# A forgetting attention that leaves its softmax undivided: the division moved to the outputs, the queries negated, the tiles moved

## The chip, the cores and the metric

The kernel is one program on one core of a Trainium2 chip. The metric is the device time of one execution in microseconds (us). A core has TensorE (PE in the profile, with PEld for its weight loads), VectorE (DVE), ScalarE (ACT), GpSimd (POOL) and SyncE (SP), which issues all of this kernel's DMAs from one in-order queue. Data lives in on-chip SBUF (128 partitions), matrix products land in PSUM (8 banks of 512 float32 in each partition), and everything else is in DRAM.

## The reference

The reference is a decoder trunk of two layers over 1024 tokens of 1024 features: convolution layer, cross-attention into 256 memory tokens, MLP; then forgetting attention, cross-attention, MLP; then a final norm. The change lies in the forgetting attention. With 16 heads of 64 features, queries `q`, keys `k`, values `v` and `c`, the cumulative sum of the log forget gates:

```python
s = jnp.einsum("bqhd,bkhd->bhqk", qi, k).astype(jnp.float32) * scale
s = s + (ci[..., :, None] - c_bhs[:, :, None, :])
s = jnp.where(mask[None, None], s, -jnp.inf)      # causal
p = jax.nn.softmax(s, axis=-1)
return jnp.einsum("bhqk,bkhd->bqhd", p.astype(v.dtype), v)
```

The result, over all heads, is multiplied by `w_o` and added to the stream. The term with `ci` is the same for a whole row and drops out of the softmax.

## The kernel before

**Number format.** Each float32 operand of a matrix product is split into a high part (ACT copies it, rounded to fp32r) and a low part (DVE subtracts: line 153, in `low`, called by `split`), and three products are summed (line 268, or 1246 in the attention's projections).

**Attention (`attend`).** The loop runs over 16 heads and, in each, over 8 blocks of 128 queries. `attention_scores` makes the scores of one block, 512 keys at a time, on PE (lines 1296 and 1297, and 1299 for the causal mask, which is added as a product with the identity). One custom DVE operation (line 1301) subtracts `cj`, the heads' gate sums broadcast over the partitions, and keeps the running row maximum `mx`. DVE negates it (`nb`, line 1304). ACT takes the exponential with that bias and sums the row into `rs` (line 1306). DVE inverts the sum (1307) and multiplies the whole row by it (1312); in odd blocks of the last two heads ACT does that (1310). `attention_transposes`, three blocks later, turns the probabilities on PE (1332) and splits them (`pth` by ACT at 156, `ptl` by DVE at 153). `attention_output`, one step after that and once for two blocks, multiplies by the values (1344, 1345), adds the two halves of the PSUM tile (1347 on ACT, 1348 on DVE) and stores `ol` to `od` in DRAM (1350). Between the blocks the loop takes three steps of `projections`, the keys, queries and values of later heads (L1246), which read the normalized stream from eight large tiles `op`.

**After it (`fox_layer`).** The eight `op` tiles are taken again for the attention's output: for each chunk `m` of 128 features (heads 2m and 2m+1) and each half of the tokens, a tile `o` is loaded from `od` (1138) and split into `op`. Then the stream is loaded again (`load_x`, line 138, from `xd`), into the place where the attention's own tiles were, and `linear_by_halves` multiplies by `w_o`: first half of the tokens for all eight output chunks, then the second half. One output chunk and half is 24 products, over eight `op` tiles in turn; its weights are two tiles `wh` and `wl`, two buffers each, and the sums go through six PSUM banks.

**What sets the order.** A planner in the compiler takes the program as traced, and issues on each engine the earliest instruction in the program that is ready by its own estimates; the order is then fixed. The MLPs are an exception: their order is written out by hand. Tiles of one tag share its buffers. The tag `t` of the pool `nrm` has four buffers of 128x512, used all over the kernel; in the attention only by `mask`, and after it by `o`. In this program each tag `t` tile is first written in the order in which the program asks for it.

**Places in SBUF.** The planner stacks the tiles of a pool in steps of 32 bytes. An unused tile `shift` of 64 bytes, set to zero at the start, stands first in the pool `nrm`. With it the tiles of `nrm`, the `op` tiles and the tiles of the MLPs begin at multiples of 128 bytes in each partition; the tiles of the attention (pool `fa`), behind the 4 bytes of `fb`, begin 32 or 96 bytes past such a multiple; the stream's tiles `x` begin 224 bytes past a multiple of 256, and the weight tiles `raw`, `wh`, `wl` 192 bytes past one.

Of the kernel before, what the change touches and what calls it, by code (L numbers as in the profile page):

```python
# [12 lines left out]
F32 = mybir.dt.float32  # L13
F32R = mybir.dt.float32r
AF = mybir.ActivationFunctionType
ALU = mybir.AluOpType
# [3 lines left out]
P = 128  # L20
D = 1024
S = 1024
NCH = D // P
HALF = 512
# [4 lines left out]
HEADS = 16  # L29
HD = 64  # L30
# [6 lines left out]
HALVES = (slice(0, HALF), slice(HALF, S))  # L37
# [49 lines left out]
def trunk(ctx, tc, a, out):  # L87
    nc = tc.nc
    act, dve, pool, pe = nc.scalar, nc.vector, nc.gpsimd, nc.tensor
# [14 lines left out]
    def col(name, i):  # L104
        return par[:, COLS[name] + i : COLS[name] + i + 1]

    def shift(p):

        dve.memset(p.tile([P, 16], F32, name="shift", bufs=1), 0.0)

    @contextmanager
    def in_order(engines=None):

# [25 lines left out]

    X = open_x()  # L140
    nrm = ctx.enter_context(tc.tile_pool(name="nrm", bufs=2))
    shift(nrm)
    opool = ctx.enter_context(tc.tile_pool(name="ops", bufs=8))
    ps = ctx.enter_context(tc.tile_pool(name="ps", bufs=2, space=PSUM))

    def bank(p):
        return p.tile([P, HALF], F32, name="mm", tag="mm")
# [7 lines left out]
    def split(hi, lo, src):  # L155
        act.copy(hi, src)  # L156
        low(lo, src, hi)
# [944 lines left out]
    def fox_layer(xd, hs, ws, seconds):  # L1102
        nonlocal X, xpool
        cd = dram.tile([HEADS, S], F32, name="cd")
        od = dram.tile([NCH, P, S], F32, name="od")

        early = {}
        with (
            tc.tile_pool(name="fs", bufs=2, space=PSUM, reuse_waits="tile") as p2,
            banks(4) as pm,  # L1110
        ):

            with in_order({mybir.EngineType.PE, mybir.EngineType.DVE, mybir.EngineType.Activation}):
# [12 lines left out]
                early["gate"] = bank(pm)[:HEADS, :]  # L1126
                product(early["gate"], by_weights(wf, hs, HALVES[0]))
                normalize(hs, None, HALVES[1], rb)
                ws.append(weights(a["wv"][0], gain="kv"))
            xpool.close()  # L1130
            xpool = ExitStack()
            with tc.tile_pool(name="fa", bufs=2) as bp:
                attend(bp, p2, pm, ws, wf, hs, early, cd, od)
        hs = operands()
        for m in range(NCH):
            for sl in HALVES:
                o = nrm.tile([P, HALF], F32, name="o", tag="t", bufs=4)
                nc.sync.dma_start(o, od[m, :, sl])
                split(*(x[:, sl] for x in hs[m]), o)
        X = open_x()  # L1140
        for sl in HALVES:
            load_x(X, xd, sl)
        with banks(6) as pm:
            linear_by_halves(pm, lambda m: weights(a["fox_wo"][m]), NCH, hs, add_to_x)

    def attend(bp, p2, pm, ws, wf, hs, early, cd, od):
        mask = nrm.tile([P, P], F32, name="mask", tag="t", bufs=4)
        make_causal_mask(nc, mask, mask_val=-1e30)
        maskr, identr = (bp.tile([P, P], F32R, name=n, bufs=1) for n in ("maskr", "identr"))
        dve.tensor_copy(maskr, mask)  # L1150
        dve.tensor_copy(identr, ident)
        tiles = {}
        project = projections(bp, ws, hs, tiles, early)
        gates = forget_gates(bp, wf, hs, cd, early)
        next(gates)
        while len(tiles) < 2:
            next(project)
            next(gates, None)
        late = []

        def run(late):
            later = []
            for n, f in late:
                if n == 0:
                    f = f()
                    if f:
                        later.append((DELAYS[1], f))
                else:
                    later.append((n - 1, f))
            return later  # L1170

        for head in range(HEADS):
            cj = bp.tile([P, S], F32, name="cj")
            nc.sync.dma_start(cj, cd[head : head + 1, :].to_broadcast([P, S]))
            for b in range(8):
                while head not in tiles:
                    next(project)
                x = attention_scores(bp, p2, tiles[head], head, b, cj, identr, maskr)
                late.append((DELAYS[0], partial(attention_transposes, bp, pm, tiles[head], head, b, x, od)))
                late = run(late)  # L1180
                for _ in range(3):
                    next(project, None)
        while late:
            late = run(late)

    def forget_gates(bp, wf, hs, cd, early):

        fb = bp.tile([HEADS, 1], F32, name="fb", bufs=1)
        nc.sync.dma_start(fb, a["fb"])
        z, e, w = (bp.tile([P, S], F32, name="x", bufs=DELAYS[0] + 1)[:HEADS, :] for _ in range(3))  # L1190
        cn = bp.tile([P, S], F32, name="cj")[:HEADS, :]
        for sl in HALVES:
            if sl.start == 0:
                t = early["gate"]
            else:
                t = bank(ps)[:HEADS, :]
                product(t, by_weights(wf, hs, sl))
            dve.tensor_scalar(z[:, sl], t, fb[:, 0:1], None, op0=ALU.add)
        yield
        act.activation(e, z, AF.Abs)  # L1200
        yield
        act.activation(e, e, AF.Exp, scale=-1.0)
# [12 lines left out]
        yield  # L1215
        dve.scalar_tensor_tensor(z, z, 0.0, cn, op0=ALU.min, op1=ALU.subtract)
        yield
        dve.tensor_tensor_scan(cn, z, z, 0.0, op0=ALU.add, op1=ALU.bypass)
        nc.sync.dma_start(cd, cn)
# [43 lines left out]

    def put_queries(bp, sl, t, qs):
        q = bp.tile([P, HALF], F32, name="q", tag="qv")
        act.activation(q, t, AF.Copy, scale=1.0 / math.sqrt(HD))  # L1266
        for i, (mine, other) in enumerate(ROWS):
            split(qs[i][mine, sl], qs[i][other, sl], q[mine, :])

# [12 lines left out]

        return transposed

    def attention_scores(bp, p2, tiles, head, b, cj, identr, maskr):

        kh, kl, qs, _, _ = tiles
        n = (b + 1) * P
        x = bp.tile([P, S], F32, name="x", bufs=DELAYS[0] + 1)
        qb = qs[:, b * P : (b + 1) * P]  # L1290
        mx = -3e38
        for j in range(0, n, HALF):
            sl = slice(j, min(j + HALF, n))
            last = sl.stop == n
            s = bank(p2)[:, : sl.stop - j]
            pe.matmul(s, qb, kl[:, sl], start=True, stop=False)  # L1296
            pe.matmul(s, qb, kh[:, sl], start=False, stop=not last)
            if last:
                pe.matmul(s[:, b * P - j :], identr, maskr, start=False, stop=True)
            m = bp.tile([P, 1], F32, name=f"mx{j}")  # L1300
            dve.tensor_tensor_reduce(x[:, sl], s, cj[:, sl], 1.0, mx, ALU.subtract, ALU.max, m)  # L1301
            mx = m
        nb = bp.tile([P, 1], F32, name="nb")
        dve.tensor_scalar(nb, mx, -1.0, None, op0=ALU.mult)  # L1304
        rs = bp.tile([P, 1], F32, name="rs")
        act.activation(x[:, :n], x[:, :n], AF.Exp, bias=nb, accum_out=rs)  # L1306
        dve.reciprocal(rs, rs)
        if head >= HEADS - 2 and b % 2:

            act.activation(x[:, :n], x[:, :n], AF.Copy, scale=rs)  # L1310
        else:
            dve.tensor_scalar(x[:, :n], x[:, :n], rs, None, op0=ALU.mult)
        return x

    def attention_transposes(bp, pm, tiles, head, b, x, od):
# [121 lines left out]
```

## Time and profile before

| what | value |
|---|---|
| median of three runs | 2830.04 us (2828.89 to 2830.18) |
| profiled execution: its own time | 2829.92 us |
| profiled execution: span in the trace | 2827.8 us |
| PE busy | 2749.2 us (97%) |
| DVE busy | 2024.9 us (72%) |
| ACT busy | 1275.5 us (45%) |
| granted TensorE clock, mean | 0.994 |

All times in the trace count from the start of its span; the run's own time is 2.1 us longer than the span. The attention runs from about 1388 us to 1893 us. The trace shows a product's duration with its latency: products of 512 columns last 393 ns, though one follows the other in less, so a busy PE can still have room. A row of the grouped view reads: line, engine, operation, output<-inputs, shape, count, then busy time and mean duration, then the engine's idle time just before, and what ended it.

### The profile page before, as it was taken

The numbers are of one execution on the slowest core, as the hardware profiler recorded it, in microseconds if no ns is written. First come the engines' busy times: TensorE is split into PE (matmuls) and PEld (weight loads), VectorE is DVE, ScalarE is ACT, GpSimd is POOL, SyncE is SP. The second block draws the span as 40 slices with busy tenths as digits, with TensorE's granted clock in tenths as the row PEclk, the third lists the DMA queues.
The fourth block names the chain that finished last, engine by engine and source line by source line (L and its number), as shares of the span: only waits on it lengthen the run. The fifth ranks groups of instructions, "written<-read, shape, count | busy, mean of one in ns | idle before, by whom it ended". The sixth has DMA issues, their size and how long they took to land.

```text
span 2827.8 us, 36219 instructions
## 1 busy us (share of the span) xinstructions
PE 2749.2 (97%) x12968; PEld 2256.6 (80%) x12968; DVE 2024.9 (72%) x3359; ACT 1275.5 (45%) x2293; POOL 705.3 (25%) x473
## 2 busy tenths in 40 slices
PE   8999999999999999999899999989999999999998
PEld 6777777888788877878588888878888888878886
DVE  5999983555766576777788888884545855577776
ACT  5112143433465553334466666673423655543332
POOL 0000000000065625774000000000000365625763
PEclk9999999999999999999999999999999999999999
DMA  6334463322164585652222222133322355565651
GB/s 219 119 119 134 124 204 119 97 90 82 53 224 177 184 303 192 215 196 88 68 73 72 65 60 59 61 120 114 97 67 102 140 187 190 196 231 195 227 201 60
DMA packets 165428, 390.68 MB, mean 138 GB/s; under 512 B 17264, under 2 KB 46192, under 8 KB 164992
## 3 DMA queue, kind: packets, MB, share of 16 engines
q1 hardware_dynamic: 165248, 388.37, 40.5%
q8 instruction: 102, 1.67, 0.2%
q14 instruction: 78, 0.64, 0.1%
HBM read 270.79 MB, written 113.31 MB: 136 GB/s over the span
## 4 chain that ended last, share of the span: by engine, by line
PE 73%; DVE 14%; ACT 5%; DMA 4%; issue 3%; SPq 0%; POOL 0%; DVEq 0%; POOLq 0%; ACTq 0%
PE mm L1066 35%; PE mm L268 27%; PE mm L1246 5%; DVE x L407 2%; DVE op L153 2%; DVE w L153 2%; PE mm L1332 1%; DVE x L1301 1%; PE mm L1344 1%; PE mm L1345 1%; DVE both L399 1%; ACT x L1306 1%; DVE wl L153 1%; DMA ua<-x 1%; PE mm L1296 1%
## 5 line engine op out<-in xcount | busy, mean ns | idle before, releaser
L1066 PE MATMUL mm<-op,w 128*128 128x512 f32 x5424 | 1253.0, 393 | 19.1 <-DVE w L153 5.7
L1066 PEld LDWEIGHTS mm<-op,w 128*128 128x128 f32 x5424 | 1019.9, 188 | 248.7 <-DVE w L153 6.5
L268 PE MATMUL mm<-op,wh 128*128 128x512 f32 x1056 | 332.4, 396 | 2.5 <-DVE op L153 2.5
L153 DVE TENSOR_TENSOR w<-r,w 128x512 fp32r<-128x512 f32 x264 | 260.9, 992 | 32.8 <-ACT w L651 32.8
L651 ACT CAST w<-r 128x512 fp32r<-128x512 f32 x264 | 162.4, 620 | 262.7 <-PE mm L1066 229.0
L268 PEld LDWEIGHTS mm<-op,wh 128*128 128x128 f32 x1056 | 200.2, 190 | 47.7 <-DVE op L153 3.8
L1246 PE MATMUL mm<-op,wh 128*128 128x512 f32 x736 | 229.5, 393 | 0.0
L153 DVE TENSOR_TENSOR w<-t,w 128x512 fp32r<-128x512 f32 x180 | 177.2, 997 | 64.7 <-ACT w L651 64.5
L268 PE MATMUL mm<-op,wl 128*128 128x512 f32 x528 | 210.5, 400 | 9.7 <-DVE x L965 8.9
L212 POOL TENSOR_TENSOR r<-v,mhalf 128x4 f32<-128x4 f32 (+1 forms) x15 | 16.8, 1117 | 749.6 <-DVE v L210 749.6
L645 POOL TENSOR_TENSOR t<-r,t 128x512 f32<-128x512 f32 x104 | 171.5, 1649 | 92.3 <-DVE w L153 65.6
L156 ACT CAST wh<-raw 128x1024 fp32r<-128x1024 f32 x96 | 100.6, 1049 | 197.6 <-PE mm L268 100.6
L863 POOL TENSOR_TENSOR x<-x,x 128x512 f32<-128x512 f32 x112 | 161.2, 1464 | 113.1 <-ACT x L876 102.3
L651 ACT CAST w<-t 128x512 fp32r<-128x512 f32 x180 | 111.7, 620 | 163.8 <-PE mm L1066 140.3
L965 DVE TENSOR_TENSOR x<-mm,x 128x512 f32<-128x512 f32 x160 | 109.4, 684 | 94.2 <-PE mm L1066 77.0
L1246 PEld LDWEIGHTS mm<-op,wh 128*128 128x128 f32 x736 | 138.7, 188 | 26.4
L268 PE MATMUL mm<-op,xsh 128*128 128x512 f32 x512 | 157.7, 392 | 0.0
L1246 PE MATMUL mm<-op,wl 128*128 128x512 f32 x368 | 154.9, 421 | 1.8 <-ACT q L1266 1.8
L156 ACT CAST pth<-mm 128x512 fp32r<-128x512 f32 (+1 forms) x224 | 105.8, 495 | 108.8 <-PE mm L555 79.7
L645 POOL TENSOR_TENSOR t<-r,r 128x512 f32<-128x512 f32 x52 | 81.7, 1571 | 292.9 <-DMA r<-in_ff_w 253.9
L407 DVE SCALAR_TENSOR_TENSOR x<-d,par,x 128x512 f32<-128x512 f32 x232 | 154.5, 745 | 0.0
L1306 ACT ACTIVATE x<-x,nb 128x128 f32<-128x128 f32 (+7 forms) x128 | 99.5, 778 | 107.7 <-DVE nb L1304 100.7
(189 smaller groups left out, 4681.8 us busy)
## 6 DMA issues: line engine op xcount, KB each, us to landing
r<-in_ff_w SPq DMA_DIRECT2D x128, 512.0 KB, 4.0
op<-ua SPq DMA_DIRECT2D x80, 512.0 KB, 6.7
us<-x SPq DMA_DIRECT2D x128, 256.0 KB, 2.9
op<-us SPq DMA_DIRECT2D x64, 512.0 KB, 5.4
raw<-mvo SPq DMA_DIRECT2D x32, 512.0 KB, 3.3
ua<-ul SPq DMA_DIRECT2D x64, 256.0 KB, 2.1
ua<-uh SPq DMA_DIRECT2D x60, 256.0 KB, 2.2
raw<-in_pw SPq DMA_DIRECT2D x24, 512.0 KB, 4.7
```

The source lines that it names most:

```text
L153: dve.tensor_tensor(lo, src, hi.bitcast(F32), op=ALU.subtract)
L156: act.copy(hi, src)
L268: pe.matmul(out_ps, x, y, start=i == 0, stop=i == len(terms) - 1)
L399: dve.scalar_tensor_tensor(both, odd[:, j : j + n], sums[:, j : j + 1], both, op0=ALU.mult, op1=ALU.add)
L407: dve.scalar_tensor_tensor(out[s], d[:, j : j + n], w, y, op0=ALU.mult, op1=ALU.add)
L645: (dve if g in (2, 3, UP, UP + 1) else pool).tensor_tensor(t, raws[g, x], raws[g, y], op=ALU.subtract)
L651: act.copy(highs[n][0], raws[steps[n][:2]])
L863: eng.tensor_tensor(u[g, x], y1, y2, op=op_)
L965: dve.tensor_tensor(v, sums[key], v, op=ALU.add)
L1066: pe.matmul(sums[key], y, z, start=first and i == 0, stop=n == last_of[key] and i == len(terms) - 1, skip_group_check=True,)
L1246: pe.matmul(t, x, y, start=n == 0, stop=n == len(terms) - 1)
L1306: act.activation(x[:, :n], x[:, :n], AF.Exp, bias=nb, accum_out=rs)
```

## The change

The scores are computed negated: `put_queries` scales by -1/8, the mask is +1e30, the DVE operation adds `cj` and keeps the row minimum, and ACT takes the exponential with scale -1 and that minimum as its bias. So the negation of the maximum falls away. The row sums go into a column of one tile `rs` of 128x16 for two heads, and neither the inversion nor the division of the rows is done there. Instead `inverse_sums`, once for two heads, inverts the 128x16 sums on DVE, transposes them on PE, copies them on ACT to a tile `ro` (of the tag `t`) and stores them to `rd` in DRAM. After the attention each tile `o` is multiplied by a tile `rs` (also of the tag `t`), which two DMAs fill, one for each head, broadcast over 64 partitions. That loop now runs over the halves outside and the chunks inside. The 64 bytes of `shift` are gone, so that `nrm`, the `op` tiles and the MLPs' tiles begin 64 bytes lower; `fb` takes 128 bytes a partition and the row minima have four buffers, so that all large tiles of the attention begin 64 bytes past a multiple of 128.

```diff
-    def shift(p):
-        dve.memset(p.tile([P, 16], F32, name="shift", bufs=1), 0.0)
...
-    shift(nrm)
...
+        rd = dram.tile([HEADS, 8, P], F32, name="rd")
...
-        for m in range(NCH):
-            for sl in HALVES:
+        for sl in HALVES:
+            for m in range(NCH):
                 o = nrm.tile([P, HALF], F32, name="o", tag="t", bufs=4)
                 nc.sync.dma_start(o, od[m, :, sl])
+                r = nrm.tile([P, HALF], F32, name="rs", tag="t", bufs=4)
+                for i in range(2):
+                    blocks = rd[2 * m + i : 2 * m + i + 1, sl.start // P : sl.stop // P, :]
+                    nc.sync.dma_start(
+                        r[i * HD : (i + 1) * HD, :], blocks.rearrange("h b q -> h (b q)").to_broadcast([HD, HALF])
+                    )
+                dve.tensor_tensor(o, o, r, op=ALU.mult)
                 split(*(x[:, sl] for x in hs[m]), o)
...
-        make_causal_mask(nc, mask, mask_val=-1e30)
+        make_causal_mask(nc, mask, mask_val=1e30)
...
+        def inverse_sums(pair, rs):
+            dve.reciprocal(rs, rs)
+            t = bank(pm)[:16, :P]
+            pe.transpose(t, rs, ident)
+            o = nrm.tile([P, HALF], F32, name="ro", tag="t", bufs=4)[:16, :P]
+            act.copy(o, t)
+            nc.sync.dma_start(rd[2 * pair : 2 * pair + 2, :, :].rearrange("h b q -> (h b) q"), o)
...
+            if head % 2 == 0:
+                rs = bp.tile([P, 16], F32, name="rs")
...
+                k = head % 2 * 8 + b
+                x = attention_scores(bp, p2, tiles[head], b, cj, identr, maskr, rs[:, k : k + 1])
...
+            if head % 2:
+                inverse_sums(head // 2, rs)
         while late:
             late = run(late)
...
-        fb = bp.tile([HEADS, 1], F32, name="fb", bufs=1)
+        fb = bp.tile([HEADS, 32], F32, name="fb", bufs=1)[:, :1]
...
-        act.activation(q, t, AF.Copy, scale=1.0 / math.sqrt(HD))
+        act.activation(q, t, AF.Copy, scale=-1.0 / math.sqrt(HD))
...
-            m = bp.tile([P, 1], F32, name=f"mx{j}")
-            dve.tensor_tensor_reduce(x[:, sl], s, cj[:, sl], 1.0, mx, ALU.subtract, ALU.max, m)
-            mx = m
-        nb = bp.tile([P, 1], F32, name="nb")
-        dve.tensor_scalar(nb, mx, -1.0, None, op0=ALU.mult)
-        rs = bp.tile([P, 1], F32, name="rs")
-        act.activation(x[:, :n], x[:, :n], AF.Exp, bias=nb, accum_out=rs)
-        dve.reciprocal(rs, rs)
-        if head >= HEADS - 2 and b % 2:
-            act.activation(x[:, :n], x[:, :n], AF.Copy, scale=rs)
-        else:
-            dve.tensor_scalar(x[:, :n], x[:, :n], rs, None, op0=ALU.mult)
+            m = bp.tile([P, 1], F32, name=f"mn{j}", bufs=4)
+            dve.tensor_tensor_reduce(x[:, sl], s, cj[:, sl], 1.0, mn, ALU.add, ALU.min, m)
+            mn = m
+        act.activation(x[:, :n], x[:, :n], AF.Exp, bias=mn, scale=-1.0, accum_out=rs)
```

More of the change, by code (lines that the diff above doesn't have):

```diff
@@ L1132, in fox_layer @@
             with tc.tile_pool(name="fa", bufs=2) as bp:
-                attend(bp, p2, pm, ws, wf, hs, early, cd, od)
+                attend(bp, p2, pm, ws, wf, hs, early, cd, od, rd)
         hs = operands()
-        for m in range(NCH):
-            for sl in HALVES:
+        for sl in HALVES:
+            for m in range(NCH):
                 o = nrm.tile([P, HALF], F32, name="o", tag="t", bufs=4)
                 nc.sync.dma_start(o, od[m, :, sl])
+                r = nrm.tile([P, HALF], F32, name="rs", tag="t", bufs=4)
[5 more added lines that the diff above has]
+                dve.tensor_tensor(o, o, r, op=ALU.mult)
                 split(*(x[:, sl] for x in hs[m]), o)
@@ L1144, in fox_layer, with attend @@
             linear_by_halves(pm, lambda m: weights(a["fox_wo"][m]), NCH, hs, add_to_x)
-    def attend(bp, p2, pm, ws, wf, hs, early, cd, od):
+    def attend(bp, p2, pm, ws, wf, hs, early, cd, od, rd):
         mask = nrm.tile([P, P], F32, name="mask", tag="t", bufs=4)
-        make_causal_mask(nc, mask, mask_val=-1e30)
+        make_causal_mask(nc, mask, mask_val=1e30)
         maskr, identr = (bp.tile([P, P], F32R, name=n, bufs=1) for n in ("maskr", "identr"))
@@ L1177, in attend @@
                     next(project)
-                x = attention_scores(bp, p2, tiles[head], head, b, cj, identr, maskr)
+                k = head % 2 * 8 + b
+                x = attention_scores(bp, p2, tiles[head], b, cj, identr, maskr, rs[:, k : k + 1])
                 late.append((DELAYS[0], partial(attention_transposes, bp, pm, tiles[head], head, b, x, od)))
@@ L1283, in put_values, with attention_scores @@
         return transposed
-    def attention_scores(bp, p2, tiles, head, b, cj, identr, maskr):
+    def attention_scores(bp, p2, tiles, b, cj, identr, maskr, rs):
         kh, kl, qs, _, _ = tiles
@@ L1290, in attention_scores @@
         qb = qs[:, b * P : (b + 1) * P]
-        mx = -3e38
+        mn = 3e38
         for j in range(0, n, HALF):
```

## The prediction

> **What bounds the kernel now.** I read the busy times first, then three stretches of the attention, then who waited for whom in them, and then the loads of the attention's output. Here are the page's first lines, and the stretches (span, then busy time and count of PE, PEld, DVE, ACT, POOL, then clock, DMA share, GB/s).
>
> ```profile
> span 2827.8 us, 36219 instructions
> PE 2749.2 (97%) x12968; PEld 2256.6 (80%) x12968; DVE 2024.9 (72%) x3359; ACT 1275.5 (45%) x2293; POOL 705.3 (25%) x473
> ```
>
> ```profile
> 1440.00:1800.00 360.00, 357.93 (x2138) 312.32 (x2137) 303.07 (x843) 220.64 (x481) 10.90 (x11) 1.00 0.21 63
> 1855.00:1893.40 38.40, 30.16 (x205) 24.70 (x203) 35.69 (x109) 33.82 (x74) 0.00 (x0) 1.00 0.24 74
> 1893.40:1938.00 44.60, 44.60 (x198) 36.63 (x198) 22.89 (x31) 15.99 (x24) 0.00 (x0) 1.00 0.54 184
> ```
>
> Three regimes stand side by side. From 1440 to 1800, with projections between the blocks, PE is busy 357.9 of 360 us: DVE at 303 has slack. From 1855, when the projections have run out, to 1893.4, PE is busy 30.2 of 38.4 us and DVE 35.7: this tail is DVE's, with ACT (33.8) close behind. From 1893.4 the product with `w_o` fills PE without a gap: some 195 products in 44.6 us, 0.229 us each. So what DVE loses before 1855 can buy no more than what PE waited for DVE there; what it loses in the tail counts.
>
> Who waited in the first stretch (total, times, longest; the PE row of L1332 is the same wait as its PEld row):
>
> ```profile
> PEld mm L1296 <- DVE mx L1301: 3.1, 6, 0.5
> PEld mm L1332 <- DVE ol L1348: 2.9, 6, 0.5
> PE mm L1332 <- DVE ol L1348: 1.5, 6, 0.3
> ```
>
> **The change, step by step.** First the main stretch. These groups of 1440 to 1800 go:
>
> ```profile
> L1312 DVE TENSOR_SCALAR x<-x,rs 128x384 f32<-128x384 f32 (+3 forms) x92 | 47.5, 517 | 2.0
> L1307 DVE RECIPROCAL rs<-rs 128x1 f32<-128x1 f32 x92 | 14.9, 162 | 32.7 <-ACT x L1306 31.5
> L1304 DVE TENSOR_SCALAR nb<-mx 128x1 f32<-128x1 f32 x92 | 13.6, 148 | 1.6
> L1332 PE MATMUL mm<-ident,x 128*128 128x128 f32 x414 | 63.3, 277 | 1.5 <-DVE ol L1348 1.5
> ```
>
> That is 76.0 us of DVE out of 303, a quarter, and almost none of it is on the path. What can come back is the 6.0 us (3.1 + 2.9) that PE's weight loads waited for DVE. I take two thirds, 4.0. Against it stand the eight transposes of `inverse_sums`, a form the trace does not have. The nearest row is L1332's: 277 ns for one is the upper end, and its busy time over its count, 63.3/414 = 0.153 us, the lower. I take 0.2 us each, 1.6 us over the attention. Sum for this stretch: -2.4, say **-2** (ends: -5 with no cost, and +2 with no gain). The adding and taking of minima instead of subtracting and maxima is the same custom operation on the same shapes, the exponential's scale and the queries' sign are operands: nothing, and there is no row from which a difference could come. The memset of `shift` is one small instruction before the span's work: nothing.
>
> **The places.** All tiles from `nrm` on move by 64 bytes. For DMAs I compare stores from the stream's tiles, 224 bytes past a multiple of 256, with those from `nrm`, on a multiple:
>
> ```profile
> ua<-uh SPq DMA_DIRECT2D x60, 256.0 KB, 2.2
> xs<-x SPq DMA_DIRECT2D x32, 256.0 KB, 2.2
> xd<-x SPq DMA_DIRECT2D x16, 256.0 KB, 2.0
> kh<-kh SPq DMA_DIRECT2D x32, 128.0 KB, 2.3
> o<-od SPq DMA_DIRECT2D x16, 256.0 KB, 2.9
> x<-xd SPq DMA_DIRECT2D x16, 256.0 KB, 5.4
> ```
>
> Same size, 2.2 against 2.2 and 2.0: no price. For PE, the scores' products (moving tiles `kh`, 32 bytes past) show no wait of their own in the lists. I take 0 for the places; what they could do in either direction goes into the width of the range, 2 us each way. The Trainium skill speaks against this move: its page "DMA: Bandwidth & Descriptors", section "How a descriptor splits into AXI transactions", says that a descriptor which starts off a 256-byte boundary pays for the bytes back to that boundary, which for rows of 2048 bytes would be 70 beats for 64. By it every store from `nrm` would last some 9% longer in its data part; the three rows above show nothing of that size in the time to landing, so the sum stays.
>
> **The tail.** From 1855 to 1893.4 these go, from there or altogether:
>
> ```profile
> L153 DVE TENSOR_TENSOR op<-o,op 128x512 fp32r<-128x512 f32 x9 | 6.1, 682 | 1.2 <-ACT op L156 1.2
> L1310 ACT ACTIVATE x<-x,rs 128x768 f32<-128x768 f32 (+3 forms) x6 | 5.4, 905 | 0.2 <-DVE nb L1304 0.2
> L156 ACT CAST op<-o 128x512 fp32r<-128x512 f32 x8 | 4.6, 626 | 1.0 <-DMA o<-od 1.0
> L1312 DVE TENSOR_SCALAR x<-x,rs 128x640 f32<-128x640 f32 (+3 forms) x6 | 3.1, 524 | 0.0
> L1307 DVE RECIPROCAL rs<-rs 128x1 f32<-128x1 f32 x12 | 1.9, 159 | 1.0 <-ACT x L1306 0.8
> L1304 DVE TENSOR_SCALAR nb<-mx 128x1 f32<-128x1 f32 x11 | 1.5, 141 | 0.0
> ```
>
> The scaling, inversion and negation are 6.5 us of DVE and 5.4 of ACT. The splits of `o` (6.1 and 4.6) leave the tail for a reason of their own. Before, the four `t` buffers were free during the attention:
>
> ```profile
> L1138 SPq DMA_DIRECT2D o<-od x16: 319/320/333, 1470.1 to 1896.5; - x16
> L156 ACT CAST op<-o x16: 606/625/651, 1847.5 to 1899.4; 128x512 fp32r<-128x512 f32 x16
> 1886.71 1.16 ACT L1306 ACTIVATE x<-x,nb 128x1024 f32<-128x1024 f32 x1
> 1896.91 0.43 SPq L138 DMA_DIRECT2D x<-xd  x1
> ```
>
> The loads began at 1470, and the splits at 1847, as the last projection let go of the `op` tiles. Now eight tiles `ro` of the same tag stand ahead of every `o` in the program, the last of them behind the last exponential. If buffers are given in program order, no `o` is loaded before that. So DVE has 12.6 us less and ACT 10.0. Consecutive DVE instructions overlap a little; I count 10 of the 12.6, which leaves 25.7, and at the old fill of 35.69/38.40 that is 27.6 us. With PE's own chains a little worse I take **29 us for 38.4, -9.4** (ends: 26 and 33). PE finishes the attention at 1893.4 - 2 - 9.4 = 1882.0.
>
> **The new wait.** The last exponential ended at 1887.9, 5.5 us before PE was done. About 1.5 of that was inversion and scaling, so it now ends 4.0 before 1882.0, at 1878.0. Inversion, transpose, copy to `ro` and their handovers (0.16, 0.28, about 0.3, and the rest between engines) take 1.4: at 1879.4 the first `o` may be loaded. One item is then: load of `o` 2.9 (row above), its two broadcast loads of 128 KB beside it (2.3 as `kh<-kh`, issued 0.32 and 0.64 later), the product with `rs` (0.68, as the DVE operation on `o`), cast 0.63, difference 0.68. First item done after 5.3. An item holds two of the four buffers, so two are in flight, each some 5 us: 2.5 us an item. The eighth, which closes the first half, is done 5.3 + 7 x 2.5 = 22.8 later, at 1902.2. In the same time the 16 loads of the stream come, 4 MB, which before were issued from 1896.9 on and landed 5.4 us after issue instead of 2.9: two rounds of items behind them cost 2 x 2.5 = 5 more: **1907.2** (ends: 0 and 9). Two loads to the two halves of the partitions are what the Trainium skill advises against ("DMA: Bandwidth & Descriptors", "Rules for kernel authors"): it says that they share the same engines, and one load over all partitions does as well. By it the pair would land like 256 KB, 2.9 after its issue, and the eight items would take about 2 us more.
>
> PE meanwhile can do what there are weights for: two output chunks, 48 products x 0.229 = 11.0 us, all but the last 6 before the eighth item. Those 6 take 1.4. Then chunk 2 waits for its weights, whose buffers were just let go: cast and difference (rows below), less what overlaps, 1.7.
>
> ```profile
> L156 ACT CAST wh<-raw 128x1024 fp32r<-128x1024 f32 x8 | 8.4, 1051 | 18.4 <-issue 10.2 <-PE mm L268 7.6 <-DMA raw<-in_fox_wo 0.6
> L153 DVE TENSOR_TENSOR wl<-raw,wh 128x1024 fp32r<-128x1024 f32 x7 | 8.6, 1224 | 3.1 <-ACT wh L156 3.1
> ```
>
> So 48 products are behind PE at 1907.2 + 1.4 + 1.7 = 1910.3; before, at 1893.4 + 11.0 = 1904.4. **Sum: +5.9 us.** The second half's eight items (another 20 us, 11 of them DVE) lie beside the other 33 us of the first half's products and cost nothing; without that cover they would cost 20. The last store to `od` no longer holds up the first half. The profiled run's own time was 2829.9, which is within 0.2 of the median: 2835.8, **2836 us**.
>
> **The rivals.** (1) *The wait is covered.* The stream's loads come after the first eight items, or the planner places them so: -5, sum +0.9, 2831. For it: before they came behind the last `o`. Against: their place comes free when the last `ol` is stored, some 5 us after 1882, while half of the items are open. (2) *The `o` loads are not held back*, because buffers go to whoever is ready. Then the tail keeps its splits and gains 6.5 on DVE but takes some nine products with `rs`, 6.2, and ends with ACT's relief, -5.4, at its best; with -2 from the main stretch, 2822.5. It decides if any `o` lands before the last exponential. Against it: the buffers would fill with `o` and `rs` at 1550 and the third `ro` would have none until the projections end, for which that very `ro` is needed. A mild form gives the same: all 6.0 us of PE's waits back, a tail of 26, no load in the way and the weights of chunk 2 in time: +0.9 - 2 - 3 - 1.7 = -5.8. (3) *Less cover.* PE has only one chunk to work on, 5.5 us instead of 11.0 (and then no wait for weights, 1.7), or the 16 loads stand before the items in SP's queue, 9 instead of 5: +9.7 or +9.9, 2840; both, 2844.
>
> **How the numbers follow.** My forecast has 0.45, (1) 0.23, (2) 0.19, (3) 0.13. A measurement of this kernel can tell about 0.2%, 5.7 us, from no change. Of the forecast's own range, 2832 to 2840, two thirds lie above 2835.7 and one third within. Slower: 0.30 + 0.13 = 0.43; same: 0.15 + 0.23 = 0.38; faster: 0.19. The range from 2822 to 2844 takes in all four, but for the farther ends of (2) and (3) with the 2 us for the places.
>
> **What would show it.** No `o<-od` before the last exponential; the tail from the last projection to the last L1345 some 29 us; then PE idle some 14 us in all over the first 48 products of L268, ended by the differences at L153 into `op`; items 2.5 us apart; no L268 wait afterwards. PE in 1440 to 1800 unchanged but for some 3 us. Wrong if `o` is loaded in the attention, if PE has no hole after it, or if products or DVE operations of one shape have other durations at the new places.

## The result and the profile after

The changed kernel takes 2860.49 us (median of four runs, 2853.51 to 2862.14) against 2830.11 for the kernel before beside it: a ratio of 1.0094 (95% interval 1.0076 to 1.0113). A second measurement gave 1.0096 (1.0082 to 1.0111). The forecast was 2836 us and its range ended at 2844, so it had the sign of its likeliest case and missed the size by 25 us.

Of the changed kernel's page, the first lines:

```profile
span 2860.1 us, 35985 instructions
PE 2750.5 (96%) x12976; PEld 2266.9 (79%) x12976; DVE 1968.7 (69%) x3006; ACT 1274.9 (45%) x2293; POOL 702.0 (25%) x473
```

DVE lost 56 us of work, and PE did the same work as before: 2750.5 us of it, spread over 32.3 us more. To see where PE stood, I cut both traces at the same events: the attention's first score to its last projection (the main stretch), on to its last product with the values (the tail), on to the first product of the second MLP. The columns are those of the prediction's stretches. The kernel before:

```profile
1402.00:1856.10 454.10, 447.41 (x2650) 389.25 (x2649) 383.58 (x1064) 279.00 (x610) 12.79 (x13) 1.00 0.23 68
1856.10:1893.70 37.60, 29.36 (x201) 24.09 (x200) 35.01 (x107) 32.77 (x70) 0.00 (x0) 1.00 0.22 68
1893.70:2175.00 281.30, 276.61 (x1344) 229.40 (x1343) 143.88 (x235) 100.21 (x179) 3.95 (x3) 1.00 0.32 106
```

And the changed kernel:

```profile
1406.10:1861.20 455.10, 450.20 (x2657) 391.43 (x2656) 312.42 (x717) 275.58 (x608) 12.30 (x13) 1.00 0.21 62
1861.20:1898.20 37.00, 29.70 (x203) 25.61 (x202) 27.71 (x73) 25.49 (x58) 0.00 (x0) 0.95 0.25 72
1898.20:2213.50 315.30, 284.23 (x1345) 232.54 (x1344) 162.56 (x263) 108.48 (x192) 3.94 (x3) 0.96 0.35 116
```

The attention has its DVE work cut by nearly a fifth and is not shorter (492.1 us, before 491.7). All the loss lies behind it: 315.3 us for 281.3. The rest of the 32.3 us is small and of both signs: the attention began 4.1 us later, and the second MLP took 6.7 us less.

What happens behind the attention, in three stretches of the changed kernel: up to the last product for which PE had weights, up to the next product, and the four us after it.

```profile
1898.20:1934.40 36.20, 27.82 (x96) 18.93 (x95) 21.84 (x32) 10.71 (x17) 0.00 (x0) 0.91 0.68 211
1934.40:1951.80 17.40, 0.14 (x1) 0.01 (x1) 8.60 (x13) 6.86 (x10) 0.00 (x0) 0.63 0.76 259
1951.80:1956.00 4.20, 4.18 (x10) 3.34 (x11) 1.11 (x1) 0.00 (x0) 0.00 (x0) 0.51 0.65 204
```

Ninety-six products, four output chunks, take 36.2 us where 96 x 0.229 = 22.0 would do, so 14.2 us are lost. The first 48 end at 1918.6, 20.4 us after the start where 11.0 would do: here the `op` tiles come in one by one. Then PE waits 3.1 us for the `wl` of the third chunk, and its next 48 products take 12.6 us, at a clock of 0.87. After them PE stands for 17.4 us. Then its clock is at 0.51, and ten products take 4.2 us instead of 2.3. These 14.2 + 17.4 + 1.9 are 33.5 of the 34.0 us. Who waited for whom from 1855 to 1965 (total, times, longest):

```profile
PE mm L263 <- DVE wl L148: 20.4, 2, 17.3
PE mm L263 <- ACT op L151: 5.2, 5, 1.6
PE mm L1169 <- DVE rs L1167: 3.7, 1, 3.7
```

The long one waits for `wl`, the low part of the weights of the fifth chunk (the other of the two is the third chunk's). Its cause stands in SP's queue, here before and then after (start, duration; a row joins loads of one kind):

```profile
1896.91 9.39 SPq L138 DMA_DIRECT2D x<-xd  x16
1906.71 1.01 SPq L252 DMA_DIRECT2D raw<-in_fox_wo  x2
```

```profile
1936.27 0.33 SPq L1134 DMA_DIRECT2D o<-od  x1
1937.65 1.09 SPq L1138 DMA_DIRECT2D rs<-rd  x2
1938.79 3.91 SPq L134 DMA_DIRECT2D x<-xd  x8
1942.74 19.41 SPq L247 DMA_DIRECT2D raw<-in_fox_wo  x5
```

In both kernels the weights of the fifth chunk come behind all outputs and all 16 loads of the stream. Before, the outputs had been loaded by 1896.9, and the weights were issued at 1906.7, while PE still had work to 1915. Now 16 outputs with 32 loads of sums stand there, most of them waiting for a buffer that an earlier one must give back, and the weights are issued at 1942.7. The weights have a wait of their own: `raw` has two buffers, and the third chunk gave one back at 1921.6, when its `wl` was made (in the kernel before at 1902.5). The other 21 us they stood behind loads that they had no need of. The mean step from one output to the next is 3.2 us, from the first of 16 differences into `op` to the last:

```profile
L148 DVE TENSOR_TENSOR op<-o,op x16: 684/692/693, 1894.3 to 1943.0; 128x512 fp32r<-128x512 f32 x16
```

In the attention's steady stretch, 1440 to 1800, the waits of PE that the prediction showed have changed places:

```profile
PEld mm L1169 <- PE mm L1265: 4.2, 6, 0.7
PEld mm L1315 <- DVE mn L1321: 1.9, 6, 0.3
PE mm L1169 <- DVE rs L1167: 1.7, 6, 0.3
```

The waits for `ol` are gone and those for the row's extreme fell from 3.1 to 1.9, but the new transposes (L1169) bring waits of their own: 1.7 us of PE for the inversion, and 4.2 of their weight loads behind projections.

### The profile page after: what moved, and what is told of

Its sections match the earlier page's. It is cut to its first block, busy times and chain, and to the rows that moved or that the text cites. A ratio compares the mean times of both kernels' runs of the same rounds, so it can differ in the third digit from the quotient of the medians.

```text
span 2860.1 us, 35985 instructions
## 1 busy us (share of the span) xinstructions
PE 2750.5 (96%) x12976; PEld 2266.9 (79%) x12976; DVE 1968.7 (69%) x3006; ACT 1274.9 (45%) x2293; POOL 702.0 (25%) x473
## 4 chain that ended last, share of the span: by engine, by line
PE 79%; DVE 9%; DMA 6%; ACT 3%; issue 2%; SPq 1%; POOL 0%; DVEq 0%; POOLq 0%; ACTq 0%
PE mm L1061 35%; PE mm L263 27%; PE mm L1265 8%; PE mm L1343 2%; DVE op L148 2%; DVE x L402 1%; DVE w L148 1%; PE mm L1355 1%; PE mm L1356 1%; PE mm L1316 1%; PE mm L1315 1%; DVE both L394 1%; DMA op<-ua 1%; DMA raw<-mqk 1%; DMA mqk<-o 1%
## 5 line engine op out<-in xcount | busy, mean ns | idle before, releaser
L263 PE MATMUL mm<-op,wl 128*128 128x512 f32 x528 | 211.9, 404 | 36.2 <-DVE wl L148 21.9
L148 DVE TENSOR_TENSOR ptl<-mm,pth 128x512 fp32r<-128x512 f32 (+1 forms) x224 | 125.4, 572 | 53.0 <-ACT pth L151 48.8
L263 PEld LDWEIGHTS mm<-op,wl 128*128 128x128 f32 x528 | 100.7, 192 | 63.8 <-issue 22.1
```

Of the source, the lines that this page charges most:

```text
L148: dve.tensor_tensor(lo, src, hi.bitcast(F32), op=ALU.subtract)
L263: pe.matmul(out_ps, x, y, start=i == 0, stop=i == len(terms) - 1)
```

## The experiments

The ratios are to the kernel before, run beside each on the same chip, with 95% intervals. "Behind" is the time from the attention's last product to the second MLP.

| run | ratio | main | tail | behind |
|---|---|---|---|---|
| before | | 454.1 | 37.6 | 281.3 |
| changed | 1.0094 (1.0076 to 1.0113) | 455.1 | 37.0 | 315.3 |
| a_again | 1.0096 (1.0082 to 1.0111) | 455.2 | 37.0 | 318.4 |
| e7_nodiv | 0.9963 (0.9947 to 0.9978) | 452.3 | 32.6 | 285.3 |
| e3_apart | 1.0032 (1.0012 to 1.0051) | 455.0 | 37.0 | 301.4 |
| e4_ro_own | 1.0043 (1.0025 to 1.0061) | 455.0 | 38.3 | 299.1 |
| e34 | 0.9993 (0.9982 to 1.0004) | 454.7 | 37.6 | 284.8 |
| e34late | 0.9982 (0.9967 to 0.9996) | 452.7 | 33.8 | 286.1 |
| b2_best | 0.9981 (0.9969 to 0.9992) | 453.7 | 33.9 | 284.0 |
| e34late_old | 1.0010 (0.9998 to 1.0022) | 452.4 | 33.5 | 286.8 |

**The changed kernel again** (a_again), no edit.

> The changed kernel a second time. Theory (its loss is the 34 us that it needs longer between the last product of the attention and the second MLP, less what the places give): 314 to 317 us there once more, the attention 492 us, 0.227 us in the MLPs, and 0.8 to 1.1% slower than before. Rival (part of the loss was of that one execution): less than 0.7%.

The attention 492.2 us, 1.0096, and 318.4 us behind, some more than expected. The loss is the kernel's, not one execution's.

**No division at all** (e7_nodiv).

```diff
-                r = nrm.tile([P, HALF], F32, name="rs", tag="t", bufs=4)
...
-                dve.tensor_tensor(o, o, r, op=ALU.mult)
...
-            if head % 2:
-                inverse_sums(head // 2, rs)
```

> The changed kernel without any division: the row sums are neither inverted nor stored, and the outputs are not multiplied by them, so the attention's result is left unnormalized. It shows what removing the softmax's division brings by itself. By the prediction (2 us in the main stretch and 9.4 in the tail): 2818 to 2822 us. Rival (DVE was not what the tail waited for, or what it gains is lost behind it): 2827 to 2831 us.

It gave 2825.63 us beside 2834.19, that is 8.6 less. Its attention:

```profile
1401.00:1853.30 452.30, 447.76 (x2650) 390.62 (x2649) 314.33 (x715) 276.89 (x607) 12.30 (x13) 1.00 0.22 67
1853.30:1885.90 32.60, 28.51 (x201) 23.97 (x201) 27.20 (x72) 25.28 (x58) 0.00 (x0) 1.00 0.20 57
```

The main stretch is 1.8 us shorter and the tail 5.0. In the tail PE is busy for 28.5 of 32.6 us: the tail was DVE's, but PE's own work (29.4 us of 37.6 in the kernel before) was a floor only 8 us below it. So the most that this change could win in the attention was 6.8 us, and 4.0 of it are lost again behind it. By its new places the run gains as well (below), so the 8.6 us are not the division's alone.

**The second half's outputs behind the first half's product** (e3_apart).

```diff
-        for sl in HALVES:
+        def outputs(sl):
...
+        outputs(HALVES[0])
         X = open_x()
-        for sl in HALVES:
-            load_x(X, xd, sl)
+        load_x(X, xd, HALVES[0])
         with banks(6) as pm:
-            linear_by_halves(pm, lambda m: weights(a["fox_wo"][m]), NCH, hs, add_to_x)
+            for sl in HALVES:
+                linear(pm, lambda m: weights(a["fox_wo"][m]), NCH, hs, add_to_x, (sl,))
+                if sl.start == 0:
+                    outputs(HALVES[1])
+                    load_x(X, xd, HALVES[1])
```

> The changed kernel with the second half's eight outputs and stream loads put in the program behind the first half's product, so that SP issues the later weights of w_o among them. Theory (the weights of the fifth output chunk stood behind all 16 outputs and 16 stream loads in SP's in-order queue): they are issued some 15 to 20 us earlier, PE's idle time of 17.3 us after the fourth chunk and the slow clock behind it go, and the time is about 2842 us. Rival (the outputs themselves, by their buffers and loads, take DVE, the DMAs and SP so that weights can't come sooner): the idle time stays or moves, and the time is 2855 us or more.

2842.60 us, and behind the attention 13.9 us less than in the changed kernel. PE's waits and SP's issues of the later weights:

```profile
PE mm L263 <- DVE wl L148: 6.5, 2, 4.4
PE mm L263 <- ACT op L151: 5.9, 5, 1.8
```

```profile
1916.02 1.47 SPq L247 DMA_DIRECT2D raw<-in_fox_wo  x2
1924.27 0.34 SPq L247 DMA_DIRECT2D raw<-in_fox_wo  x1
```

The fifth weights are issued at 1916.0 instead of 1942.7, and the two waits for `wl`, 20.4 us in all, have become two of 6.5. SP's order was the cause of that part. The other part, the slow arrival of the first half's outputs, stays.

**The sums in a buffer of their own tag** (e4_ro_own).

```diff
-            o = nrm.tile([P, HALF], F32, name="ro", tag="t", bufs=4)[:16, :P]
+            o = bp.tile([HD, 2 * P], F32, name="ol")[:16, :P]
```

> The changed kernel with the transposed sums in a buffer of tag ol instead of tag t, so that loads of the outputs need not wait for the last sums. By the prediction's step (the buffers of tag t, given in program order, hold every o back until the last exponential): the first o is loaded in the attention, the splits begin as the projections end, the first half is complete some 8 to 12 us sooner, and as the weights of the fifth chunk still stand behind all outputs, the time falls by about 8 to 14 us, to some 2848 to 2854 us. Rival (the order of SP alone sets it): the fifth weights come when they did, and the time stays at 2860 us, within 3.

2844.45 us, and 16.2 us less behind the attention. Where the outputs were loaded, first in the changed kernel and then in this run:

```profile
L1134 SPq DMA_DIRECT2D o<-od x16: 325/394/577, 1883.8 to 1936.3; - x16
```

```profile
L1134 SPq DMA_DIRECT2D o<-od x16: 319/326/584, 1465.0 to 1909.0; - x16
```

And this run's longest wait of PE:

```profile
PE mm L263 <- DVE wl L148: 15.0, 1, 15.0
```

The buffers of tag `t` do hold the outputs back, as the prediction had it. With the sums elsewhere the first output is loaded at 1465.0, the first half is complete when the attention ends, and the 14.2 us are gone; the wait for the fifth weights, 15.0 us, is left.

**Both edits** (e34), the two diffs above together.

> The changed kernel with both edits: the second half's outputs behind the first half's product, and the transposed sums in a buffer of tag ol. Theory (two separate losses, the outputs held back by tag t and the weights behind all outputs in SP's queue): from the last product of the attention to the second MLP 282 to 285 us, where the changed kernel had 315.3 and each edit alone 301.4 and 299.1; no wait of PE for weights over 3 us; 2830 us by the first profile of before, that is 0.1% above or below it. Rival (one loss, which either edit moves): 295 us or more.

0.9993, and 284.8 us behind the attention: two separate losses, each undone by its own edit. PE still stood 3.7 us in the tail (`PE mm L1174 <- DVE rs L1172`).

**The transposes of the sums later** (e34late).

```diff
             if head % 2:
-                inverse_sums(head // 2, rs)
+                late.append((3, partial(inverse_sums, head // 2, rs)))
```

> As the run with both edits, and the inversion of the sums goes into the list of late steps, so that their transposes stand behind the transposes of the last block in PE's order. Theory (in the attention's tail PE stood 3.7 us at the transposes of the sums, which wait for the last exponential, with products behind them): the attention's tail of 37 us becomes 33 to 34 us, and the time falls 3 to 4 us below that of both edits. Rival (PE would have waited there for the last probabilities anyway): the tail stays at 36 to 38 us.

The tail is 33.8 us instead of 37.6 (and the main stretch 2.0 shorter), so this wait did cost time. In the changed kernel one sees it directly (start, duration, idle time and its releaser):

```profile
1884.71 0.69 DVE L148 TENSOR_TENSOR ptl<-mm,pth 128x512 fp32r<-128x512 f32 x1 [0.23 <-ACT pth L151]
...
1887.16 0.19 ACT L1323 ACTIVATION_READ_ACCUMULATOR x<-x,mn 128x1 f32 x1
1887.37 0.25 DVE L1167 RECIPROCAL rs<-rs 128x16 f32<-128x16 f32 x1 [1.10 <-ACT x L1323]
1887.78 0.37 PE L1169 MATMUL mm<-ident,rs 128*16 128x128 f32 x1 [3.67 <-DVE rs L1167]
1887.80 0.56 PE L1355 MATMUL mm<-ptl,vs 128*128 128x256 f32 x1
```

The small transpose stands ahead of products with the values whose `ptl` was made by 1885.4. What the tail had won by the missing division it lost here.

**The stream's loads one by one** (b2_best).

```diff
...
+                def get(m):
+                    w = weights(a["fox_wo"][m])
+                    nc.sync.dma_start(X[:, m, sl], xd[:, m, sl])
+                    return w
...
```

> The mended kernel of the last three edits with new places, and each load of the stream put in the program behind the weights of its own output chunk, so that the weights' place in SP's queue is not behind all eight. Theory (the 4.6 us that it still loses between the attention and the second MLP are a wait of 3.2 us for weights and a slower clock behind it): that wait goes, 281 to 283 us from the last product of the attention to the second MLP, and some 2822 us. Rival (the weights wait for their buffers, not for SP): 285 us or more, and the time stays.

The wait of 3.2 us is gone, and 284.0 us are left behind the attention, where 281 to 283 were expected; 2824.62 us, 0.9981. Of the 2.7 us that still part it from the kernel before there, I did not look for the cause.

**The same with the old places** (e34late_old), to the kernel of e34late:

```diff
...
+    shift(nrm)
...
-        fb = bp.tile([HEADS, 32], F32, name="fb", bufs=1)[:, :1]
+        fb = bp.tile([HEADS, 1], F32, name="fb", bufs=1)
```

> The mended kernel of the last three edits, but with the places of the kernel before: 64 bytes set aside and the gate's bias 4 bytes wide. Theory (its gain of 0.18% over before came from the places, 5 to 13 us, and the division on the outputs, mended, costs what it saves): 2831 to 2838 us, a ratio of 1 to 1.003. Rival (the division moved and mended is worth the 5 us that the attention became shorter): a ratio of 0.998 or less, as with the new places.

1.0010 against 0.9982, with about the same attention (485.9 us, against 486.5). So mended the division on the outputs is worth nothing that can be measured against the kernel before: the 5.8 us that its attention gains are lost behind it, 286.8 us for 281.3. That the places make the whole difference to e34late is likely but not shown: 0.28% is about what the next two runs, one and the same kernel measured twice, differ by.

**The places alone** (e1_places, e1_again), to the kernel before:

```diff
-    shift(nrm)
...
-        fb = bp.tile([HEADS, 1], F32, name="fb", bufs=1)
+        fb = bp.tile([HEADS, 32], F32, name="fb", bufs=1)[:, :1]
```

> The kernel before with the places of the changed one and nothing else of it: the 64 bytes are dropped and the gate's bias takes 128 bytes a partition. Theory (places cost nothing, all the loss is at the start of the product with w_o): 2830 us, within 2 us, and 0.229 us from one 512-column product to the next in the attention and in both MLPs. Rival (the moved tiles slow loads or products): some 5 to 30 us more, spread over the MLPs or the convolution, with longer products or longer times to landing there.

> The kernel before with the new places alone, a second time. Theory (the moved tiles let the products of the MLPs follow each other every 0.227 us instead of 0.229, as its first profile had it): a ratio of 0.995 to 0.998 again, and 0.227 us from one of the MLPs' products to the next. Rival (the first ratio, 0.9968, came from single executions whose MLPs waited less): 1 within 0.1%, though the products' step may be 0.227 us again, lost in longer waits.

0.9968 (0.9954 to 0.9981) and 0.9995 (0.9982 to 1.0008): the first faster, the second not distinguishable. The two intervals do not overlap although the kernel is the same, so ratios from two measurements can differ by 0.3%. **The kernel before, again** (c0_before):

> The kernel before, unchanged, as a second profile of it and as a test of how finely two programs can be told apart. Theory (what differs between kernels outside the attention and the product with w_o is a matter of single executions: three short waits of PE in each MLP, and a lower clock after the longer ones): a ratio of 1 within 0.3%, and MLPs of other lengths than the 635.1 and 636.9 us of the first profile, anywhere from 628 to 640. Rival (the places set these lengths): both MLPs again within 1 us of 635.1 and 636.9.

1.0004 (0.9992 to 1.0017), and MLPs of 635.7 and 637.4 us, within 1 us of the first profile, as the rival had it. But the places do not set these lengths alone: the first MLP lasted 628.0 us in e1_places and 638.7 in e1_again. What the places do change is seen in the same 160 us of the first MLP, 850 to 1010, in which PE never waits. Before, changed, and with 128 bytes set aside (e8_shift128):

```profile
L1066 PE MATMUL mm<-op,w 128*128 128x512 f32 x701 | 160.6, 391 | 0.0
```

```profile
L1061 PE MATMUL mm<-op,w 128*128 128x512 f32 x708 | 160.6, 389 | 0.0
```

```profile
L1066 PE MATMUL mm<-op,w 128*128 128x512 f32 x690 | 160.5, 395 | 0.0
```

A row of products that never waits is busy for the steps between them and one product's own duration. So (160.6 - 0.39)/700 = 0.2289 us is the step from one product to the next, then (160.6 - 0.39)/707 = 0.2266, and (160.5 - 0.39)/689 = 0.2324.

```diff
-        dve.memset(p.tile([P, 16], F32, name="shift", bufs=1), 0.0)
+        dve.memset(p.tile([P, 32], F32, name="shift", bufs=1), 0.0)
```

> The kernel before with 128 bytes set aside instead of 64, so that the tiles of nrm, the op tiles and the MLPs' tiles begin 64 bytes past a multiple of 256 (before: on a multiple of 256; changed: 192 past one) and the attention's tiles 64 higher too. Theory (the products' step depends on the place modulo 128 bytes): 0.227 us in the MLPs, and some 0.3% faster than before. Rival (it depends on the place relative to the weights' tiles, which stand 192 past a multiple of 256, or modulo 256): 0.229 us, and no change.

It took 1.0089 (1.0071 to 1.0108), 2852.41 us beside 2830.24: 64 bytes more cost 22 us. The theory, the place modulo 128 bytes, fell; the rival had named the distance from the weights, but expected no change. The next two runs moved the weights, w0_weights with 64 bytes in front of them and w1_both64 with 128:

```diff
-    shift(nrm)
+    shift(wp)
```

> The kernel before with its 64 bytes set aside in front of the weights' tiles instead of in front of nrm: weights on a multiple of 256 bytes, and everything from nrm on where it was, also on a multiple of 256. Theory (what counts is how far the moving tiles stand from the weights' modulo 256: 64 bytes gave 0.229 us, none 0.227, 128 bytes 0.232): 0.227 us from one of the MLPs' products to the next. Rival (the moving tiles' own place modulo 256 counts: on a multiple 0.229, 192 past it 0.227, 64 past it 0.232): 0.229 us, as before. In time either is 2825 to 2831 us.

> The kernel before with 128 bytes set aside in front of the weights: weights, nrm, op tiles and the MLPs' tiles all begin 64 bytes past a multiple of 256. Theory (the distance from the weights counts): 0.227 us in the MLPs, and 2825 to 2831 us. Rival (the moving tiles' own place counts): 0.232 us and some 2852 us, as the run with 128 bytes in front of nrm.

```profile
L1066 PE MATMUL mm<-op,w 128*128 128x512 f32 x707 | 160.4, 389 | 0.0
```

That is w0_weights, (160.4 - 0.39)/706 = 0.2266 us; w1_both64 has 708 in 160.6, again 0.2266. In both the moving tiles stand where they had given 0.229 and 0.232. So it is not their own place that counts, but how far it is from that of the weights, modulo 256 bytes: none 0.227, 64 apart 0.229, 128 apart 0.232. (The three placements with 0.227 have one and the same distance, so that it counts modulo 256, and not by a longer period, is taken from where the tiles lie and not tested.) The times: 0.9963 (0.9950 to 0.9977), and 0.9966 (0.9953 to 0.9979). w0_weights, 2820.90 us in its one measurement, has the lowest median here: one line moved, nothing else of the change.

**One load of the sums for each output** (e5_onedma).

```diff
-                for i in range(2):
-                    blocks = rd[2 * m + i : 2 * m + i + 1, sl.start // P : sl.stop // P, :]
-                    nc.sync.dma_start(
-                        r[i * HD : (i + 1) * HD, :], blocks.rearrange("h b q -> h (b q)").to_broadcast([HD, HALF])
-                    )
+                blocks = rd[2 * m : 2 * m + 2, sl.start // P : sl.stop // P, :]
+                nc.sync.dma_start(r, blocks.rearrange("h b q -> h (b q)").unsqueeze(1).to_broadcast([2, HD, HALF]))
```

> The changed kernel with the two broadcast loads of the sums for an output, one to each half of the partitions, made one load to all 128. The Trainium skill (DMA: Bandwidth & Descriptors, Rules for kernel authors) has it that two halves share the same engines and gain nothing, so that one load does as well; by it, with one issue less of 0.5 us in SP's queue for each of 16 outputs, the outputs follow each other in about 2.8 us instead of 3.2, the weights of the fifth chunk come 6 us sooner, and the time is 2852 to 2856 us. Rival (one load of 256 KB lands later than two of 128 KB): 3.2 us or more for an output, and 2860 us or more.

2913.99 us, 1.0290. While only such a load runs, the DMA share (the column before the last) is this:

```profile
1902.00:1904.00 2.00, 1.26 (x6) 0.71 (x4) 0.00 (x0) 0.00 (x0) 0.00 (x0) 0.97 0.13 42
1908.50:1912.00 3.50, 1.22 (x3) 0.40 (x2) 0.69 (x1) 0.48 (x1) 0.00 (x0) 0.50 0.13 50
```

0.13 is two of 16 engines: the pattern of the source has 2 as its outermost size, and the load runs on two. The Trainium skill says just this ("DMA: Bandwidth & Descriptors", "Rules for kernel authors", the rule on using all 16 engines: an outermost size below 16 confines the whole load to that many), and the trace agrees. The rule on two halves that the prediction weighed remains untried: a single load that spreads over all engines was not among the runs.

## Why the prediction was wrong, step by step

Between the two spans lie 32.3 us, where the prediction summed to 5.9. From the attention's last product to the second MLP it had 17.3 more (48 products done 28.3 us after 1882.0 instead of 11.0 after 1893.4), and 34.0 were measured; from the attention it had 11.4 less, and 0.4 more were measured. The rest, -2.1, is the later start and the shorter second MLP.

- **The step that failed** is "the second half's eight items lie beside the other 33 us of the first half's products and cost nothing". PE's products were there, but the weights for them stood behind those items in SP's queue. The step named DVE's 11 us in them and not their 24 loads, nor what SP issues after those. It cost the wait of 17.4 us and about 2 us of slow clock behind it, 19 us where 0 was said; e3_apart took 13.9 us back, and both edits together (e34) 30.5 of the 34.0.
- "Two output chunks" of weights ready was right, and so was the wait of the next chunk for its split: 3.1 us, with "1.7" said. But two more chunks lay loaded in `raw`, so PE had 96 products before it lacked weights altogether, and "no L268 wait afterwards" was wrong there.
- "2.5 us an item", the first half complete at 1907.2: 3.2 us an item, and the eighth difference ended at 1917.4, or 1913.3 counted from the same start of the attention. "Some 14" us idle over the first 48 products came out as 9.4 lost; that the loss over 96 products is 14.2 is a coincidence.
- "29 us for 38.4, -9.4" in the tail: 37.0 for 37.6. Without any division it is 32.6. The step scaled DVE's work and left PE's own 28.5 to 30 us as no floor; and the transposes were priced at 0.2 us each, while the last of them held PE for 3.7 us. What is queued behind a waiting instruction was not asked of PE here, as it was not asked of SP's later weights above.
- Main stretch, "-2" with -4.0 for DVE's work and +1.6 for the transposes: without division -1.8, with the transposes +1.0, so they and their waits cost 2.8 us.
- "I take 0 for the places": they take 2.3 ns of 229 from each product of the MLPs, 12 us over 5424 of them. Part of it seems to return as longer waits in the MLPs (below): over the seven runs at equal distance whose start of `w_o` was as before or mended, the ratio lay between 0.9963 and 0.9995. The prediction compared only DMAs and looked for waits; the step between products stood in the trace of before, but with nothing to compare it to.
- Against the rule on 256-byte boundaries that the prediction weighed it was right to stay with the rows: the stores from `nrm` (`ua<-uh`) landed 2.27 us after issue at the median, before 2.22, that is 2% later. How long the data part alone took, these landings do not tell.
- That `o` is held back by tag `t`, that PE would wait at the start of the product with `w_o`, and the sign were right. "No `o<-od` before the last exponential" was not quite: the first was issued at 1883.8, and that exponential began at 1886.1. Its sums, however, stood in SP's queue behind the last `rd<-ro`, issued at 1888.5.

## What to carry to other kernels

Before work is moved behind a stage, list what the in-order DMA queue has to issue after it, and ask when the first load behind it is needed: here loads that wait for buffers held up weights for 21 us after their own buffer was free. A tile from a shared tag is a place in line; a small temporary with a tag that later work uses holds all of that work back. Removing a quarter of an engine's work gains at most the distance to the next floor in the stretch where that engine ends last, and a tiny instruction that depends on the last result belongs behind, not ahead of, ready products in the same queue.

## What was not expected of the hardware

The step between products of 512 columns that wait for nothing depends on where the moving tile stands relative to the weights' tile, modulo 256 bytes: in the MLPs 0.2266 us at the same offset (in three placements, 0, 64 and 192 past a multiple), 0.2289 at 64 bytes, 0.2324 at 128. In this kernel 128 bytes apart cost 0.89% of the whole time against 64 apart. Why is open; no run tried distances below 64, or 192. The attention does not show it: its projections' products follow each other every 0.231 us (median) before and after alike.

The MLPs did not become shorter in step with it: in the profiles at equal distance one lasts from 627.3 to 639.5 us, with the old places 634.2 to 638.9. Their waits differ from one execution to the next, and a longer one costs twice, by the clock. In the first MLP of the changed kernel (639.5 us) PE's longest waits from 720 to 1360, and the two stretches of 20 us that hold the waits of 3.3 and 4.2 us:

```profile
PE mm L1061 <- ACT m L948: 4.2, 1, 4.2
...
PE mm L1061 <- DVE x L807: 3.3, 1, 3.3
```

```profile
780.00:800.00 20.00, 16.75 (x67) 13.43 (x67) 18.97 (x18) 11.27 (x21) 17.12 (x11) 0.88 0.90 320
1040.00:1060.00 20.00, 16.89 (x64) 13.75 (x65) 16.84 (x25) 13.18 (x21) 0.23 (x1) 0.83 0.76 265
```

The clock falls to 0.88 and 0.83 there; in the kernel before, whose waits at these two places were 1.1 and 2.8 us, it stayed at 1.00. The Trainium skill ("TensorE: Matmul & The Clock Gate", "HAM oscillation — how this bites in real kernels") warns of idle gaps above some 3.4 us. The waits of 4.2 and 17.3 us agree, but these traces show no such bound: the one of 3.3 us lowered the clock, and so did shorter ones. In the kernel before another wait of 2.8 us, ending at 2501, left the clock at 0.83 from 2500 to 2510, and in w0_weights waits of 2.1 and 2.3 us, near 1067 and 2528, were each followed by a clock of 0.83 over ten us. What decides between two waits of 2.8 us, one with and one without, stays open here.
